# A state space layer's decays: step sizes as logarithms in the exponent, directions merged by a predicated copy out of PSUM

## The chip, the cores and the metric

The kernel runs on one core of a Trainium2 chip. A core has five engines that run their own instruction streams side by side: TensorE (PE, with its weight loads PEld), VectorE (DVE), ScalarE (ACT), GpSimd (POOL) and SyncE (SP, which here issues all DMAs). They wait for each other through semaphores, and each works through its own stream strictly in order. The metric is the time of one execution on the device in microseconds (us).

## The reference

The program is a two-layer encoder over 512 positions of width 1024. Layer 0 mixes tokens by retention and neighbourhood attention, layer 1 by a bidirectional state space (SSD) mixer; a GeGLU block follows each. The change touches only the SSD mixer:

```
dt = softplus(dt_raw + dt_bias)            # per position, direction, head
A = -exp(a_log)
log_a = dt * A
v_f = xh * dt[:, :, 0]                     # forward direction
v_b = xh * dt[:, :, 1]                     # backward direction
y = bidir_scan(qc, kb, v_f, v_b, log_a[:, :, 0], log_a[:, :, 1])
y = y + xh * d_skip
y = y * silu(z)
y = rms_norm per group(y) * norm_g
return y @ w_out

# chunked_scan, one direction, chunks of 128 positions
cs = cumsum(log_a)
decay = exp(where(mask, cs_j - cs_l, -inf))
y_intra = einsum((q k^T) * decay, v)
y_inter = (q . h) * exp(cs)
```

There are 32 heads in 4 groups of 8, head width 64, state width 128. Within a chunk, position j of a head receives from position l the weight (q_j . k_l) exp(cs_j - cs_l) dt_l: from l up to j by the forward direction's cs and dt, from l behind j by the backward direction's. The two halves of this 128x128 matrix never overlap, so one matrix per chunk and head holds both directions.

## The kernel before

The stage of the layer (`mixer1`) works channel-major: weights come in units of 128x1024 by DMA (`wst`), ScalarE casts them to their high part (`whi`, L81), VectorE subtracts it for the low part (`wlo`, L82), and three matmuls (L86 to L88) form one product in near full precision. Projections (`project`) go into the four PSUM buffers of the pool `mm`. A second PSUM pool, `px`, has four buffers as well, and everything else of this layer goes round in them: transposes (`pt`), `pg`, the chunk states (`st`), the part of y from earlier chunks (`pi`), the part from within a chunk (`py`), and the sums of squares (`pss`).

`steps` (L587 to L652) computes dt, the running sums `pf` of the logarithms of the decays and the weights `sw` of the chunk states, with (direction, head) on partitions; it writes `pf` to DRAM (`pd`) and transposes `pf`, `dt` and `sw` into `tok`, positions on partitions. `ddt` is the difference of the two directions' dt.

`head(o, j)` (L730 to L747) builds the matrix of one head, for four chunks at once (128x512). It loads two rows of `pd`, broadcast over the partitions (`pb`, forward and backward). Per chunk, ScalarE forms the forward exponent in `e` (L741), VectorE the backward one and the larger of the two (L742, the right one in each half), and ScalarE the matrix of step sizes `ds` from the triangular mask `um` (L744). Then follow Exp over all four chunks (L745), the product with `gt`, the transposed q k^T of the group (L746), and the product with `ds` (L747). `pair(o, q)` multiplies the matrices of two heads with the tokens (`py`, L782), adds `y` from `inter` (`pi` L762, `ti` L766), multiplies by the silu of `z` (L786), squares (L788), splits the result into `yh` and `yl` (L794, L795) and adds up the squares on POOL (L792). `rms` turns them into `pss` (L802), and `out_tile` projects the group out.

What is written in which order stands in the table `SLOTS`, one row per group: G is the products, s a state, h a head, i `inter`, p a pair, t and n a projection of this or the next group, S and N their silus, o an out projection of the group before, r `rms`. The row of the last group:

```
"t9 G h0 s0 s1 o0 t8 h4 s2 h2 i0 t6 o1 t7 S h1 h3 p0 i1 p1 i2 i3 h5 p2 h6 h7 p3"
```

A scheduler then orders the instructions of each engine by their place in this writing, by the buffers that are free, and by priorities (the splits of weights are moved ahead). The order on each engine is fixed when the kernel is built; on the chip an engine waits where the next instruction's inputs or buffers aren't ready. A tile of a pool waits for the last reader of the tile that had its buffer before.

Of the kernel before, what the change touches and what calls it, by code (L numbers as in the profile page):

```python
# [7 lines left out]
F32 = mybir.dt.float32  # L8
R32 = mybir.dt.float32r
BF16 = mybir.dt.bfloat16  # L10
AF = mybir.ActivationFunctionType
ALU = mybir.AluOpType
PSUM = bass.MemoryType.PSUM
# [2 lines left out]
P = 128  # L16
S = 512
NT = S // P
# [517 lines left out]
SSD_H = NG * HPG  # L536
# [16 lines left out]
def mixer1(E, w_dt, w_fm, cw, dtc, cols, mask, w_out, g_post_row, done):  # L553
# [4 lines left out]
    nc, tc = E.nc, E.tc  # L558
    C = P
    H, H2 = SSD_H, 2 * SSD_H  # L560
    with ExitStack() as ctx:
        pool = lambda name, bufs: ctx.enter_context(tc.tile_pool(name=name, bufs=bufs))
        one, two, four = pool("m1", 1), pool("m1b", 2), pool("m1d", 4)

        few = pool("m1s", 1)
# [4 lines left out]
        um = one.tile([P, P], F32, name="um")  # L570
# [7 lines left out]
            nc.sync.dma_start(xd[t], E.x[:, t, :])  # L578


        tok = one.tile([P, 3, NT, H2], F32, name="tok")
        ddt = one.tile([P, NT, H], F32, name="ddt")
        etot = one.tile([P, H2, NT], F32, name="etot")
        pd = E.dram.tile([H2, S], F32, name="pd")
        yd = E.dram.tile([H2, S], F32, name="yd")
# [1 line left out]
        def steps():  # L587
# [7 lines left out]
            for k in range(KD):  # L595
                c = slice(k * H2, k * H2 + H2)
                E.mm3(ps[:H2], wh[:, c], wl[:, c], E.xh[:, k], E.xl[:, k], k == 0, k == KD - 1)
            bc = few.tile([P, 2], F32, name="bc")
            nc.sync.dma_start(bc, dtc)
            nc.scalar.activation(bc[:, 1:2], bc[:, 1:2], AF.Exp)  # L600
            nc.vector.tensor_scalar(bc[:, 1:2], bc[:, 1:2], -1.0, None, op0=ALU.mult)
# [6 lines left out]
            with tc.tile_pool(name="lp", bufs=1) as lpp:  # L608
                dt = lpp.tile([P, 256], F32, name="dt")
                sw = lpp.tile([P, 256], F32, name="sw")  # L610
                ysc = lpp.tile([P, 256], F32, name="ysc")
                msk = half("msk")
                lp = log1p_exp_neg(E, lambda n: lpp.tile([P, 256], F32, name="lp_" + n), z)
                nc.vector.scalar_tensor_tensor(dt, z, 0.0, lp, op0=ALU.max, op1=ALU.add)
                nc.vector.tensor_scalar(la, dt, bc[:, 1:2], None, op0=ALU.mult)
                nc.vector.memset(msk, 1.0)
                nc.vector.memset(chunks(msk)[:, :, 0:1], 0.0)
                nc.vector.tensor_tensor_scan(pf, msk, la, 0.0, op0=ALU.mult, op1=ALU.add)
                ones = lpp.tile([P, P], F32, name="ones")
                diag = lpp.tile([P, 2, P], F32, name="diag")  # L620
                tot = lpp.tile([P, 2, 1], F32, name="tot")
                nc.vector.tensor_copy(tot, chunks(pf)[:, :, C - 1:C])
                for i in range(2):
                    r = slice(i * H2 + H, i * H2 + H2)
                    nc.vector.tensor_tensor(pf[r], pf[r], la[r], op=ALU.subtract)
                nc.vector.tensor_tensor(chunks(tm), tot.broadcast_to([P, 2, C]), chunks(pf), op=ALU.subtract)
                et = lpp.tile([P, 2], F32, name="et")
                nc.scalar.activation(et, tot.rearrange("p c o -> p (c o)"), AF.Exp)

                nc.vector.memset(ones, 1.0)  # L630
                for c in range(2):
                    nc.vector.tensor_scalar(diag[:, c], E.ident, et[:, c:c + 1], None, op0=ALU.mult)
                pe = E.px.tile([P, 2, P], F32, name="pe", tag="px")
                nc.tensor.matmul(pe.rearrange("p c n -> p (c n)"), ones, diag.rearrange("p c n -> p (c n)"),
                                 start=True, stop=True)
                nc.scalar.copy(etot.rearrange("p h (i c) -> p c i h", i=2), pe.rearrange("p c (i h) -> p c i h", i=2))
                for i in range(2):
                    r = slice(i * H2, i * H2 + H2)
                    nc.sync.dma_start(pd[:, i * 256:i * 256 + 256], pf[r])
                    f, b = slice(i * H2, i * H2 + H), slice(i * H2 + H, i * H2 + H2)  # L640
                    nc.scalar.activation(ysc[f], pf[f], AF.Exp)
                    nc.scalar.activation(ysc[b], tm[b], AF.Exp)
                    nc.scalar.activation(sw[f], tm[f], AF.Exp)
                    nc.scalar.activation(sw[b], pf[b], AF.Exp)
                    nc.sync.dma_start(yd[:, i * 256:i * 256 + 256], ysc[r])
                nc.vector.tensor_tensor(sw, sw, dt, op=ALU.mult)
                for i, s in enumerate((pf, dt, sw)):
                    pt = E.px.tile([P, 2, 2, H2], F32, name="pt", tag="px")
                    for c in range(2):
                        nc.tensor.transpose(pt[:, c].rearrange("p i h -> p (i h)"), s[:, c * C:(c + 1) * C], E.ident)  # L650
                    nc.scalar.copy(tok[:, i].rearrange("p (i c) h -> p c i h", i=2), pt)
            nc.vector.tensor_tensor(ddt, tok[:, 1, :, :H], tok[:, 1, :, H:], op=ALU.subtract)  # L652

        def rows(i, dr, g, c):
            o = dr * H + g * HPG
            return tok[:, i, c, o:o + HPG].rearrange("p (h o) -> p h o", o=1).broadcast_to([P, HPG, 64])
# [55 lines left out]
        def state(o, dr, i):  # L712

            g = o["g"]
            c = i if dr == 0 else NT - 1 - i
            xs = E.tmp.tile([P, 512], F32, name="xs", tag="tmp")
            nc.vector.tensor_tensor(hv(xs), hv(o["x"][:, c]), rows(2, dr, g, c), op=ALU.mult)
            ps = E.px.tile([P, 512], F32, name="st", tag="px")
            nc.tensor.matmul(ps, o["bt"][:, c], xs, start=True, stop=True)  # L719
            ns = one.tile([P, 512], F32, name=f"state{dr}{i}")  # L720
# [9 lines left out]
        def head(o, j):  # L730

            g = o["g"]
            h = g * HPG + j
            pb = [three.tile([P, S], F32, name="pb", bufs=3) for _ in range(2)]
            for dr in range(2):
                nc.sync.dma_start(pb[dr], pd[dr * H + h].partition_broadcast(P))
            e = three.tile([P, NT, C], F32, name="e")
            ds = ys.tile([P, NT, C], F32, name="ds")
            for c in range(NT):
                cc = slice(c * C, (c + 1) * C)  # L740
                nc.scalar.activation(e[:, c], pb[0][:, cc], AF.Identity, scale=-1.0, bias=tok[:, 0, c, h:h + 1])  # L741
                nc.vector.scalar_tensor_tensor(e[:, c], pb[1][:, cc], tok[:, 0, c, H + h:H + h + 1], e[:, c],  # L742
                                               op0=ALU.subtract, op1=ALU.max)
                nc.scalar.activation(ds[:, c], um, AF.Identity, scale=ddt[:, c, h:h + 1], bias=tok[:, 1, c, H + h:H + h + 1])  # L744
            nc.scalar.activation(e, e, AF.Exp, scale=-1.0)  # L745
            nc.vector.tensor_tensor(e, e, o["gt"], op=ALU.mult)  # L746
            o["m"][j] = e, nc.vector.tensor_tensor(e, e, ds, op=ALU.mult)  # L747

        def inter(o, q):

# [228 lines left out]
def _layouts(np, i):  # L979
# [19 lines left out]
    cw = np.concatenate([i["c_conv_w"][0], i["c_conv_b"][0][None]])  # L999
    xw, bw, cw = cw[:, :2048].reshape(6, NG, 4, P), cw[:, 2048:2560].reshape(6, NG, 1, P), cw[:, 2560:].reshape(6, NG, 1, P)  # L1000
    a["c_cw"] = np.concatenate([bw, cw, xw], 2).transpose(3, 1, 2, 0)
    a["c_dtc"] = np.tile(np.stack([i["c_dt_bias"][0].reshape(-1), i["c_a_log"][0].reshape(-1)], 1), (2, 1))
    d = np.repeat(i["c_d_skip"][0].reshape(4 * NG, 2), 64, 1)
    a["c_cols"] = np.stack([d.T, i["c_norm_g"][0].reshape(4 * NG, P).T], 1)
    a["c_mask"] = np.triu(np.ones((P, P), np.float32))
# [37 lines left out]
```

## Time and profile before

| | us |
|---|---|
| time, median of 3 runs | 1435.91 (1434.77 to 1436.99) |
| the profiled execution's own time | 1435.64 |
| its span, first to last instruction | 1433.9 |
| the SSD mixer in it | about 655 to 1065 |

TensorE's mean granted clock is 0.994 of full speed. Over the layer's stretch, 655 to 1066 us, TensorE is busy 396.6 us of 411, VectorE 355.5 and ScalarE 283.7. The page of the profile counts 1486 instructions on VectorE and 1192 on ScalarE in the whole program, 128 of each of the three per-chunk operations of `head` among them. Matmuls of 128x512 are pipelined: one shows 0.39 us, while the next starts 0.23 us after it, so busy times on TensorE are a union of overlapping spans. In rows of the timeline the first number is the start, the second the duration, and the brackets name how long the engine had been idle and what ended that.

### The profile page before, as it was taken

The page shows a single profiled execution, that of the slowest core. Times are in us where ns is not written, and L with a number is a line of the kernel's source. Part 1 is how long each engine was busy: PE and PEld are TensorE (multiplying, and loading weights), DVE is VectorE, ACT ScalarE, POOL GpSimd, SP SyncE. Part 2 cuts the span into 40 slices and gives each one's busy share as a digit, 9 for nine tenths or more (in the row PEclk, how much of TensorE's full clock was granted, in tenths as well). Part 3 has the DMA queues.
Part 4 walks back from the last instruction along what each step waited for, and adds up shares of the span by engine and source line. Part 5 has one row for each costly group of instructions (what it writes and reads, how often), then busy time and mean ns, then how long its engine had stood idle before and what let it go on. Part 6 is the DMA issues. An engine that isn't in the chain of part 4 may idle for free.

```text
span 1433.9 us, 18004 instructions
## 1 busy us (share of the span) xinstructions
PE 1400.5 (98%) x6832; PEld 1144.0 (80%) x6832; DVE 945.2 (66%) x1486; ACT 718.4 (50%) x1192; POOL 61.4 (4%) x67
## 2 busy tenths in 40 slices
PE   7999999999999999999999999999889999999998
PEld 6877777898888888888778787777678888888886
DVE  6478888666566552457789886998986666564232
ACT  4346666444444431334887866676644444443230
POOL 0010110100000000000000000000110000000000
PEclk9999999999999999999999999999999999999999
DMA  7443232232332333423565354354532333323221
GB/s 283 148 132 101 85 96 77 86 105 89 103 93 99 101 93 100 131 84 107 144 190 172 121 172 142 93 153 154 152 114 83 100 101 91 103 90 102 88 103 59
DMA packets 56950, 166.34 MB, mean 116 GB/s; under 512 B 7200, under 2 KB 7968, under 8 KB 56864
## 3 DMA queue, kind: packets, MB, share of 16 engines
q1 hardware_dynamic: 56864, 165.20, 36.4%
q8 instruction: 54, 0.88, 0.2%
q14 instruction: 32, 0.26, 0.1%
HBM read 157.57 MB, written 5.51 MB: 114 GB/s over the span
## 4 chain that ended last, share of the span: by engine, by line
PE 88%; DVE 4%; ACT 3%; DMA 2%; issue 2%; POOL 0%; SPq 0%; DVEq 0%; POOLq 0%; ACTq 0%
PE mm L86 27%; PE mm L87 26%; PE mm L88 26%; PE pi L762 1%; DMA pb<-pd 1%; PE st L719 1%; PE py L782 1%; PE pt L140 1%; PE y L449 1%; PE sc L433 1%; DVE wlo L82 0%; PE pt L663 0%; PE sc L434 0%; DMA x<-in_x 0%; ACT whi L81 0%
## 5 line engine op out<-in xcount | busy, mean ns | idle before, releaser
L88 PE MATMUL mm<-xl,whi 128*128 128x512 f32 (+2 forms) x1216 | 463.4, 381 | 3.0 <-DVE xl L82 3.0
L86 PE MATMUL mm<-xh,whi 128*128 128x512 f32 (+1 forms) x1216 | 464.5, 382 | 1.4 <-ACT bf L692 1.2
L87 PE MATMUL mm<-xh,wlo 128*128 128x512 f32 (+2 forms) x1216 | 462.8, 381 | 0.0
L82 DVE TENSOR_TENSOR wlo<-wst,whi 128x1024 fp32r<-128x1024 f32 (+1 forms) x208 | 256.0, 1231 | 125.2 <-ACT whi L81 120.6
L81 ACT CAST whi<-wst 128x1024 fp32r<-128x1024 f32 (+1 forms) x208 | 216.5, 1042 | 125.9 <-PE mm L87 96.3
L88 PEld LDWEIGHTS mm<-xl,whi 128*128 128x128 f32 (+1 forms) x1216 | 229.0, 188 | 47.2 <-DVE xl L82 3.2
L86 PEld LDWEIGHTS mm<-xh,whi 128*128 128x128 f32 x1216 | 229.2, 188 | 46.2 <-ACT bf L692 1.6
L87 PEld LDWEIGHTS mm<-xh,wlo 128*128 128x128 f32 (+1 forms) x1216 | 229.0, 188 | 42.7 <-issue 0.6
L227 DVE SCALAR_TENSOR_TENSOR cv<-mm,cwt,cv 128x511 f32<-128x511 f32 x88 | 66.0, 750 | 148.9 <-ACT cv L226 148.9
L226 ACT ACTIVATE cv<-mm,cwt 128x512 f32<-128x512 f32 x88 | 68.7, 780 | 128.0 <-PE mm L88 128.0
L86 PE MATMUL mm<-whi,hh 128*128 128x512 f32 x288 | 112.0, 389 | 0.0
L87 PE MATMUL mm<-whi,hl 128*128 128x512 f32 x288 | 112.0, 389 | 0.0
L88 PE MATMUL mm<-wlo,hh 128*128 128x512 f32 x288 | 112.0, 389 | 0.0
L81 ACT CAST hh<-cv 128x512 fp32r<-128x512 f32 x44 | 27.3, 621 | 103.3 <-DVE cv L235 103.3
L228 DVE SCALAR_TENSOR_TENSOR cv<-mm,cwt,cv 128x511 f32<-128x511 f32 x88 | 66.0, 750 | 3.0
L86 PEld LDWEIGHTS mm<-whi,hh 128*128 128x128 f32 x288 | 54.1, 188 | 11.3
L87 PEld LDWEIGHTS mm<-whi,hl 128*128 128x128 f32 x288 | 54.1, 188 | 11.2
L88 PEld LDWEIGHTS mm<-wlo,hh 128*128 128x128 f32 x288 | 54.1, 188 | 11.2
L744 ACT ACTIVATE ds<-um,tok,ddt 128x128 f32<-128x128 f32 x128 | 55.3, 486 | 11.9 <-DVE e L747 11.8
L741 ACT ACTIVATE e<-pb,tok 128x128 f32<-128x128 f32 x128 | 43.1, 392 | 16.6 <-DMA pb<-pd 14.6
L82 DVE TENSOR_TENSOR hl<-cv,hh 128x512 fp32r<-128x512 f32 x44 | 30.5, 693 | 28.9 <-ACT hh L81 28.9
L683 DVE SCALAR_TENSOR_TENSOR xf<-mm,cwt,xf 128x511 f32<-128x511 f32 (+1 forms) x64 | 47.2, 741 | 3.1 <-ACT xf L680 2.9
(236 smaller groups left out, 1932.8 us busy)
## 6 DMA issues: line engine op xcount, KB each, us to landing
wst<-in_f_up SPq DMA_DIRECT2D x88, 512.0 KB
wst<-in_f_down SPq DMA_DIRECT2D x44, 512.0 KB
wst<-in_c_fm SPq DMA_DIRECT2D x40, 512.0 KB
pb<-pd SPq DMA_DIRECT2D x64, 256.0 KB
wst<-in_ab_fm SPq DMA_DIRECT2D x20, 512.0 KB
gain<-yd SPq DMA_DIRECT2D x32, 256.0 KB
wst<-in_c_out SPq DMA_DIRECT2D x16, 512.0 KB
gain<-in_norms SPq DMA_DIRECT2D x8, 512.0 KB
```

What stands on the lines that cost most here:

```text
L81: self.nc.scalar.copy(hi, src)
L82: self.nc.vector.tensor_tensor(lo, src, hi.bitcast(F32), op=ALU.subtract)
L86: mm(out, lh, rh, start=first, stop=False)
L87: mm(out, ll, rh, start=False, stop=False)
L88: mm(out, lh, rl, start=False, stop=last)
L140: nc.tensor.transpose(pt[:, j], xs[:, j * P:(j + 1) * P], self.ident)
L226: nc.scalar.activation(o, ps, AF.Identity, scale=w(1), bias=w(3))
L227: nc.vector.scalar_tensor_tensor(o[:, 1:], ps[:, :S - 1], w(0), o[:, 1:], op0=ALU.mult, op1=ALU.add)
L228: nc.vector.scalar_tensor_tensor(o[:, :S - 1], ps[:, 1:], w(2), o[:, :S - 1], op0=ALU.mult, op1=ALU.add)
L683: nc.vector.scalar_tensor_tensor(r[:, a], ps[:, b], wc(j), r[:, a], op0=ALU.mult, op1=ALU.add)
L741: nc.scalar.activation(e[:, c], pb[0][:, cc], AF.Identity, scale=-1.0, bias=tok[:, 0, c, h:h + 1])
L744: nc.scalar.activation(ds[:, c], um, AF.Identity, scale=ddt[:, c, h:h + 1], bias=tok[:, 1, c, H + h:H + h + 1])
```

## The change

In `steps` the step sizes are floored at 1e-20, their logarithm is taken (a new activation, Ln), and `sign * pf + ln dt` is formed, with the sign -1 for the forward and +1 for the backward direction, which comes as a third column with the biases. This sum and `sw` are the two planes of `tok` that are left; `dt` itself and `ddt` are no longer transposed or formed. In `head` ScalarE now adds the token's column to the broadcast rows, once per direction and chunk: the backward exponent in place in its `pb`, the forward one into a PSUM tile `ea` of the pool `px`. One predicated copy on VectorE overwrites the backward exponent with the forward one where the mask `um`, read as integers, isn't zero. Exp and the product with `gt` follow; the product with `ds` is gone, since dt is in the exponent. `pb` has five buffers for three. Operations per head: ScalarE eight of 128x128 and one Exp, as before; VectorE one copy and one product of 128x512 for four operations of 128x128 and two of 128x512.

```diff
-        tok = one.tile([P, 3, NT, H2], F32, name="tok")
-        ddt = one.tile([P, NT, H], F32, name="ddt")
+
+        tok = one.tile([P, 2, NT, H2], F32, name="tok")
...
-            bc = few.tile([P, 2], F32, name="bc")
+            bc = few.tile([P, 3], F32, name="bc")
...
-                for i, s in enumerate((pf, dt, sw)):
+                ex = lpp.tile([P, 256], F32, name="lp_e")
+                nc.vector.tensor_scalar(ex, dt, 1e-20, None, op0=ALU.max)
+                nc.scalar.activation(ex, ex, AF.Ln)
+                nc.vector.scalar_tensor_tensor(ex, pf, bc[:, 2:3], ex, op0=ALU.mult, op1=ALU.add)
+                for i, s in enumerate((ex, sw)):
...
-            nc.vector.tensor_tensor(ddt, tok[:, 1, :, :H], tok[:, 1, :, H:], op=ALU.subtract)
...
-            nc.vector.tensor_tensor(hv(xs), hv(o["x"][:, c]), rows(2, dr, g, c), op=ALU.mult)
+            nc.vector.tensor_tensor(hv(xs), hv(o["x"][:, c]), rows(1, dr, g, c), op=ALU.mult)
...
-            pb = [three.tile([P, S], F32, name="pb", bufs=3) for _ in range(2)]
+            pb = [three.tile([P, NT, C], F32, name="pb", bufs=5) for _ in range(2)]
             for dr in range(2):
                 nc.sync.dma_start(pb[dr], pd[dr * H + h].partition_broadcast(P))
+
+            first = E.px.tile([P, NT, C], F32, name="ea", tag="px")
+            for dr in (1, 0):
+                for c in range(NT):
+                    nc.scalar.activation((first, pb[1])[dr][:, c], pb[dr][:, c], AF.Identity, scale=1.0 - 2 * dr,
+                                         bias=tok[:, 0, c, dr * H + h:dr * H + h + 1])
+            nc.vector.copy_predicated(pb[1], um.bitcast(U32).rearrange("p (o l) -> p o l", o=1).broadcast_to([P, NT, C]), first)
             e = three.tile([P, NT, C], F32, name="e")
-            ds = ys.tile([P, NT, C], F32, name="ds")
-            for c in range(NT):
-                cc = slice(c * C, (c + 1) * C)
-                nc.scalar.activation(e[:, c], pb[0][:, cc], AF.Identity, scale=-1.0, bias=tok[:, 0, c, h:h + 1])
-                nc.vector.scalar_tensor_tensor(e[:, c], pb[1][:, cc], tok[:, 0, c, H + h:H + h + 1], e[:, c],
-                                               op0=ALU.subtract, op1=ALU.max)
-                nc.scalar.activation(ds[:, c], um, AF.Identity, scale=ddt[:, c, h:h + 1], bias=tok[:, 1, c, H + h:H + h + 1])
-            nc.scalar.activation(e, e, AF.Exp, scale=-1.0)
-            nc.vector.tensor_tensor(e, e, o["gt"], op=ALU.mult)
-            o["m"][j] = e, nc.vector.tensor_tensor(e, e, ds, op=ALU.mult)
+            nc.scalar.activation(e, pb[1], AF.Exp)
+            o["m"][j] = e, nc.vector.tensor_tensor(e, e, o["gt"], op=ALU.mult)
...
-    a["c_dtc"] = np.tile(np.stack([i["c_dt_bias"][0].reshape(-1), i["c_a_log"][0].reshape(-1)], 1), (2, 1))
+    sign = np.repeat(np.array([-1, 1], np.float32), SSD_H)
+    a["c_dtc"] = np.tile(np.stack([i["c_dt_bias"][0].reshape(-1), i["c_a_log"][0].reshape(-1), sign], 1), (2, 1))
```

The lines of the changed kernel stand a few further down (L741 and L744 become L745, L745 becomes L749, L746 becomes L750, the copy is L747, and from there on three are added). What the change moves on the engines is read from the built order at three places.

**ScalarE, first heads of group 0**, ahead of the first `py`. Before: the last operations of the third head, two casts, the table of Exp, three Exps, and the silus of `z`.

```order
L744 ACTIVATE ds<-um,tok,ddt 128x128
L81 CAST whi<-wst 128x1024
L741 ACTIVATE e<-pb,tok 128x128 x4
L81 CAST whi<-wst 128x1024
L745 ACT_TABLE_LOAD
L745 ACTIVATE e<-e 128x512 x3
L689 ACT_TABLE_LOAD
L689 ACTIVATE z<-mm 128x512
```

Now, at the same place:

```order
L745 ACTIVATE pb<-pb,tok 128x128 x3
L745 ACTIVATE ea<-pb,tok 128x128 x8
L82 CAST whi<-wst 128x1024
L749 ACT_TABLE_LOAD
L749 ACTIVATE e<-pb 128x512 x2
L745 ACTIVATE pb<-pb,tok 128x128 x4
L693 ACT_TABLE_LOAD
L693 ACTIVATE z<-mm 128x512
```

The eight writes of `ea` for two heads stand in a block ahead of a cast and of Exp, and the third head's Exp has moved behind the silus.

**ScalarE, end of group 2**, where the last pair's square goes to `pss`. Before, ten operations of two heads stand ahead of the square:

```order
L680 ACTIVATE xf<-mm,cwt 128x512
L81 CAST whi<-wst 128x1024
L744 ACTIVATE ds<-um,tok,ddt 128x128 x8
L741 ACTIVATE e<-pb,tok 128x128 x2
L788 ACTIVATE sq<-y 128x512
L794 ACTIVATE yh<-y,col 128x512
L81 CAST whi<-wst 128x1024
```

Now:

```order
L749 ACTIVATE e<-pb 128x512
L82 CAST whi<-wst 128x1024
L745 ACTIVATE pb<-pb,tok 128x128 x4
L82 CAST whi<-wst 128x1024
L791 ACTIVATE sq<-y 128x512
L797 ACTIVATE yh<-y,col 128x512
L693 ACT_TABLE_LOAD
```

Four operations of one head are left there, ahead of a cast.

**ScalarE, tail of group 3**, from the last silus of `z` on. Before, the last Exp stands ahead of the silus' table, and no head is left behind them:

```order
L745 ACTIVATE e<-e 128x512
L689 ACT_TABLE_LOAD
L689 ACTIVATE z<-mm 128x512
L692 ACTIVATE z<-mm 128x512 x3
L788 ACTIVATE sq<-y 128x512
L81 CAST whi<-wst 128x1024
L788 ACTIVATE sq<-y 128x512
L794 ACTIVATE yh<-y,col 128x512 x2
L788 ACTIVATE sq<-y 128x512
L794 ACTIVATE yh<-y,col 128x512
L788 ACTIVATE sq<-y 128x512
L794 ACTIVATE yh<-y,col 128x512
```

Now, behind the four silus, a square, a cast of `wo`, one `ea`, a square and two `yh`:

```order
L745 ACTIVATE ea<-pb,tok 128x128
L82 CAST whi<-wst 128x1024
L745 ACTIVATE ea<-pb,tok 128x128 x2
L749 ACT_TABLE_LOAD
L749 ACTIVATE e<-pb 128x512
L745 ACTIVATE pb<-pb,tok 128x128 x4
L745 ACTIVATE ea<-pb,tok 128x128 x8
L791 ACTIVATE sq<-y 128x512
L797 ACTIVATE yh<-y,col 128x512
L749 ACTIVATE e<-pb 128x512 x2
L791 ACTIVATE sq<-y 128x512
L797 ACTIVATE yh<-y,col 128x512
```

Most of head 5 and all of heads 6 and 7 now stand behind the silus of `z`, with a table load of Exp of their own. Across the program ScalarE loads a table 38 times, 36 before.

More of the change, by code (lines that the diff above doesn't have):

```diff
@@ L10 @@
 BF16 = mybir.dt.bfloat16
+U32 = mybir.dt.uint32
 AF = mybir.ActivationFunctionType
```

## The prediction

> **What bounds the kernel now.** I read the page's busy shares first, then the table of windows for the state space layer (655 to 1065 us, the only stage that the diff touches), then TensorE's waits in it, then the groups by line, and last the timeline round each wait.
>
> The page's busy shares (share of the span, instructions), and the first line of its chain of waits:
>
> ```profile
> PE 1400.5 (98%) x6832; PEld 1144.0 (80%) x6832; DVE 945.2 (66%) x1486; ACT 718.4 (50%) x1192; POOL 61.4 (4%) x67
> ...
> PE 88%; DVE 4%; ACT 3%; DMA 2%; issue 2%; POOL 0%; SPq 0%; DVEq 0%; POOLq 0%; ACTq 0%
> ```
>
> A row of the table of windows: stretch, its length, busy us of TensorE, its weight loads, VectorE, ScalarE and POOL, granted clock, DMA share and GB/s:
>
> ```profile
> 920.00:940.00 20.00, 20.00 (x112) 16.21 (x108) 19.99 (x31) 14.55 (x27) 1.30 (x1) 1.00 0.75 227
> ```
>
> TensorE's waits in this layer: what it waited for, us in total, times, the longest:
>
> ```profile
> PE py L782 <- DVE e L747: 2.8, 1, 2.8
> PE py L782 <- DVE ti L766: 2.1, 2, 1.8
> ...
> PE pss L802 <- POOL sq L792: 1.4, 1, 1.4
> ...
> PE mm L87 <- DVE yl L795: 1.1, 2, 0.6
> ```
>
> TensorE is the bound: 98% busy, 88% of the chain that ended last. From 920 to 940 VectorE is busy 19.99 us of 20, and TensorE still 20.00. So a microsecond taken off VectorE is worth nothing by itself; what the change can win is TensorE's waits on this layer's decays: 2.8 + 2.1 + 1.4 + 1.1 = 7.4 us, and what the clock adds to them, in windows right behind the waits that end at 722.46, 966.61 and 1025.51:
>
> ```profile
> 723.10:726.40 3.30, 3.30 (x22) 2.97 (x17) 2.51 (x4) 1.99 (x6) 0.00 (x0) 0.50 0.46 145
> 968.90:972.10 3.20, 3.20 (x9) 2.48 (x8) 1.89 (x3) 2.93 (x6) 0.09 (x1) 0.50 0.49 138
> ...
> 1026.90:1030.20 3.30, 3.12 (x18) 2.11 (x18) 3.30 (x4) 1.93 (x4) 2.33 (x1) 0.50 0.62 168
> ```
>
> Behind each of the three longest waits stands a stretch at clock 0.50. Over 3.3 us at half speed at most 1.65 us is lost. The ceiling is thus about 7.4 + 3 x 1.65 = 12 us, under 1% of the span. The Trainium skill, "TensorE: Matmul & The Clock Gate", section "What's actually happening", lets the clock fall to half after an idle window of about 3.4 us; here waits of 1.4 to 2.8 us were enough, so the trace decides. By the page's rule those stretches would be worth nothing to the sum.
>
> **The change, head by head.** 32 heads, by the groups of ScalarE and then VectorE in this layer (count | busy us, mean ns of one | idle before them and its cause):
>
> ```profile
> L81 ACT CAST whi<-wst 128x1024 fp32r<-128x1024 f32 x54 | 56.3, 1044 | 9.4 <-PE mm L88 4.2 <-PE mm L87 3.3 <-issue 1.1
> L744 ACT ACTIVATE ds<-um,tok,ddt 128x128 f32<-128x128 f32 x128 | 55.3, 486 | 11.9 <-DVE e L747 11.8
> L741 ACT ACTIVATE e<-pb,tok 128x128 f32<-128x128 f32 x128 | 43.1, 392 | 16.6 <-DMA pb<-pd 14.6 <-PE py L782 2.0
> ```
>
> ```profile
> L82 DVE TENSOR_TENSOR wlo<-wst,whi 128x1024 fp32r<-128x1024 f32 x53 | 65.6, 1238 | 4.6 <-ACT whi L81 4.5
> ...
> L742 DVE SCALAR_TENSOR_TENSOR e<-pb,tok,e 128x128 f32<-128x128 f32 x128 | 39.1, 353 | 4.8 <-DMA pb<-pd 4.8
> L747 DVE TENSOR_TENSOR e<-e,ds 128x512 f32<-128x512 f32 x32 | 21.6, 681 | 0.1
> L746 DVE TENSOR_TENSOR e<-e,gt 128x512 f32<-128x512 f32 x32 | 21.4, 682 | 4.4 <-ACT e L745 4.4
> L795 DVE SCALAR_TENSOR_TENSOR yl<-y,col,yh 128x512 fp32r<-128x512 f32 x16 | 17.2, 1089 | 0.7 <-ACT yh L794 0.7
> ...
> L785 DVE TENSOR_TENSOR y<-py,y 128x512 f32<-128x512 f32 x16 | 10.8, 683 | 0.8 <-PE py L782 0.8
> ```
>
> VectorE spends (39.1 + 21.6 + 21.4) / 32 = 2.57 us a head now; afterwards one multiply, 0.68, and one predicated copy of 128x512 with its data in PSUM. No row has such a copy. Bounds: 0.35 us (the small row above) and 1.09 us (yl, the dearest row of that size). The nearest row is L785, same size, one operand in PSUM: I take 0.68. So 1.36 us, 1.2 less a head, 39 us in all, nearly all of it under TensorE's cover.
>
> ScalarE swaps four ds of 486 ns for four of the L741 kind at 392 that write PSUM. No row writes PSUM from ScalarE; I take 0.32 (the step of a row of L741 back to back) to 0.42 us each, since each ea waits for the one before it in the same PSUM tile. That is 0 to 0.6 us a head less. The new cost is a place: ea takes one of the four "px" buffers of PSUM, which pi, py, st and pss share, from its first write to the predicated copy. SP gets no new kind of work: with five pb buffers the loads of two heads are issued without a wait, which shortens ScalarE's 14.6 us of waiting for pb; at a DMA share of 0.75 and less there is room for them. ScalarE's wait was hidden, so: 0.
>
> **Steps section.** Two transposes of 0.11 us fewer on TensorE: -0.2. The Ln needs a table load of its own, and Exp another one after it. Both stand on ScalarE where it waited 1.83 us for pf:
>
> ```profile
> 690.58 0.42 ACT L641 ACTIVATE ysc<-pf 32x256 f32<-32x256 f32 x1 [1.83 <-DVE pf L618]
> ```
>
> The second load (1.28) and the Ln (about 0.42 as this row) fit into 1.83: 0; if they don't, what is late is a cast of whi, +1 at most.
>
> **First heads of group 0.** The timeline there (start, us, engine, line, operation; in brackets the idle time before it and what ended it):
>
> ```profile
> 710.80 0.68 DVE L727 TENSOR_TENSOR state<-st,state 128x512 f32<-128x512 f32 x1
> ...
> 715.29 1.28 ACT L745 ACT_TABLE_LOAD   x1
> ...
> 716.59 1.15 ACT L745 ACTIVATE e<-e 128x512 f32<-128x512 f32 x2
> ...
> 719.03 0.39 PE L87 MATMUL mm<-xh,wlo 128*128 128x512 f32 x1
> 719.26 0.39 PE L88 MATMUL mm<-xl,whi 128*128 128x512 f32 x1
> ...
> 722.46 1.45 PE L782 MATMUL py<-e,xt 128*64 128x128 f32 x16 [2.81 <-DVE e L747]
> ...
> 723.84 2.84 PE L762 MATMUL pi<-cf,state 128*128 128x128 f32 x12
> ```
>
> After the change the first ea must wait for a px buffer that a state addition frees, about 711.5 (710.80 + 0.68). Then 8 x 0.42, a cast of 1.04 and the table load of 1.28: the two Exps run 717.2 to 718.4, and the second multiply ends at 719.1. TensorE arrives at 719.6 (722.46 - 2.81). The wait goes, and with it up to 1.4 us of half clock (twelve pi take 2.84 us at clock 0.50, so half of it at full speed): -2 to -4, taken -3.
>
> **Ends of groups 1 and 2.** The timeline at the end of group 2, ahead of its pss:
>
> ```profile
> 960.70 3.19 ACT L744 ACTIVATE ds<-um,tok,ddt 128x128 f32<-128x128 f32 x8
> ...
> 962.96 0.68 DVE L786 TENSOR_TENSOR y<-y,z 128x512 f32<-128x512 f32 x1
> ...
> 963.80 0.69 ACT L741 ACTIVATE e<-pb,tok 128x128 f32<-128x128 f32 x2
> 964.39 0.62 ACT L788 ACTIVATE sq<-y 128x512 f32<-128x512 f32 x1
> ...
> 965.15 1.41 POOL L792 TENSOR_TENSOR sq<-sq 128x512 f32<-128x512 f32 x1 [19.45 <-ACT sq L788]
> 966.61 1.05 PE L802 MATMUL pss<-mean,sq 128*128 128x1 f32 x8 [1.40 <-POOL sq L792]
> ```
>
> Here y stood ready at 963.64 (962.96 + 0.68), but eight ds and two e were queued ahead of its square: 0.75 us. After the change four pb and a cast are left ahead of it (the second place of the order), which need not wait for y; and 20 matmuls instead of 17 lie between py and pss, 0.23 us each (the two matmuls above). Group 1 goes the other way, 15 matmuls instead of 24. Together I take -1.5 (0 to -3).
>
> **New waits for px.** In groups 1 and 2 the pi of a pair now take buffers that an ea gives back. A pi that is late by one predicated copy costs 0.3 to 0.7 us; behind it on TensorE stand the projections' matmuls, so it is paid in full. Two or three such: +1 (0.5 to 2).
>
> **Tail of group 3.** This decides the sign. The timeline from the last silus of z to pss:
>
> ```profile
> 1021.30 1.28 ACT L689 ACT_TABLE_LOAD   x1
> ...
> 1024.06 1.57 ACT L692 ACTIVATE z<-mm 128x512 f32<-128x512 f32 x3
> ...
> 1025.50 0.65 ACT L788 ACTIVATE sq<-y 128x512 f32<-128x512 f32 x1
> 1025.51 1.09 PE L782 MATMUL py<-e,xt 128*64 128x128 f32 x16 [1.75 <-DVE ti L766]
> ...
> 1026.97 1.98 PE L782 MATMUL py<-e,xt 128*64 128x128 f32 x16 [0.37 <-DVE ti L766]
> 1027.48 1.34 ACT L794 ACTIVATE yh<-y,col 128x512 fp32r<-128x512 f32 x2
> ...
> 1040.63 0.95 PE L802 MATMUL pss<-mean,sq 128*128 128x1 f32 x8
> ```
>
> Before, no Exp stands behind the silu's table load at 1021.30, and both py wait only for a px buffer, which ti frees behind the silu of z. Now the ea of heads 5 to 7 need such buffers too, so they stand behind that silu on ScalarE, and Exp must be loaded once more. Added up from 1025.50: sq 0.5, wo 0.5, ea 0.4, sq 0.5, two yh 1.3, ea 0.4, whi 1.05, two ea 0.8, table load 1.28, Exp 0.6: 1032.8. VectorE has y 0.55, wo 0.68 and wlo 1.22 between the copy (behind the last ea, done 1031.6) and the multiply, which ends at 1034.8: py of pair 2 is 9.3 us late. ScalarE's four pb (1.3) and eight ea (3.3) end at 1037.4. The square waits for py 1.7, y + py 0.68 and y times z 0.68, to 1037.9; with yh it is 1039.1, after two Exps 1040.3, after the multiply 1041.0. Then py 1.7, y + py 0.68, y times z 0.68, sq 0.6 and POOL's sum 1.4: pss at 1046.1 against 1040.63, +5.5. The out matmuls (38 before pss then, 36 now) fill TensorE's wait and are no gain. Bounds: +3.5 (ea at 0.32, the wlo late) to +7.5 (copies at 1.09, a pi more in the way). If the first ea got their buffers before the silu, it would be 0.
>
> The Trainium skill, "ScalarE: Activation LUTs", section "What ACT_TABLE_LOAD costs", speaks against this change: a switch of tables costs 1283 ns and a drain of about 1380 more. The trace has the 1283 ns, and no drain: 715.29 + 1.28 is 716.57, and the Exp starts at 716.59. With the page's drain the sum would be an estimated 1.4 us higher.
>
> **Sum**, against the profiled execution's 1435.64: -0.2 - 3 - 1.5 + 1 + 5.5 = +1.8. The median of the runs is 0.27 above that execution, so I forecast 1435.91 + 1.8 = **1437.7 us**.
>
> **Rivals.** (1) Faster: the tail doesn't stretch. VectorE is 1.2 us a head quicker, so px buffers come free sooner and the last ea get theirs before the silu; ScalarE's order is fixed, which speaks against it. 1437.7 - 5.5 = 1432.2, and 1430 with the ends at their best. (2) Slower: ScalarE's queue stops at an ea that has no buffer, with casts of whi behind it. It decides as soon as a stop outlasts the matmuls whose weights are split already, a unit of 12 at 0.23 us being 2.8 us. A stop of twice that, 5.6, costs 2.8 us; one in each of groups 1 and 2: 1437.7 + 5.6 = 1443.3. For it: there are four px buffers, and two can be held by ea. Against it: casts of whi wait for TensorE to give back buffers (9.4 us idle, 7.5 of it put down to matmuls), so they run ahead now. (3) It does nothing: the new waits eat what the first heads give, the tail pays half: 1435 to 1437.
>
> **Chances.** Forecast 0.45 (its own range 1434.5 to 1441), rival 1 0.25, rival 2 0.2, rival 3 0.1. Range 1430 to 1445. A measurement of this kernel tells about 0.2% from no change, 2.9 us: faster is under 1433.0, slower over 1438.8. Faster 0.25 (rival 1 mostly); same 0.37 (0.24 of the forecast, rival 3, and the rest of rival 1); slower 0.38 (0.18 of the forecast, rival 2).
>
> **What will show it.** The wait of py at 722 gone, its twelve pi in about 1.4 us; the predicated copy at 0.68 us in its group; one more Exp table load behind the last silu of z, py of pair 3 some 14 us later, and pss about 5.5 us later after the end of the last z projection. Wrong, if ea in group 3 run ahead of the silu, if the copy costs over 1.1 us, or if casts of whi gain idle time put down to VectorE.

## The result, and the profile after

The changed kernel takes 1445.69 us, the median of 5 runs (1442.88 to 1448.37), against 1435.91 (1434.36 to 1437.08) of the kernel before: a ratio of 1.0072, 95% interval 1.0058 to 1.0086. It is slower by about 10 us, above the range of the forecast.

The profiled execution took 1446.27 us, its span is 1444.5 (before 1433.9), 10.6 us more. TensorE's timeline shows where they arose, at places that both kernels have:

| first matmul of | before | after | difference | gained since the place above |
|---|---|---|---|---|
| pss, group 0 | 787.84 | 785.40 | -2.44 | -2.44 |
| pg, group 2 | 896.58 | 897.68 | +1.10 | +3.54 |
| pi behind the last z projection | 1023.37 | 1025.01 | +1.64 | +0.54 |
| pss, group 3 | 1040.63 | 1049.85 | +9.22 | +7.58 |
| end of the span | 1433.9 | 1444.5 | +10.6 | +1.38 |

The page's busy shares of the kernel after: TensorE does the same work, VectorE 31.8 us less (945.2 before), ScalarE 7.4 less.

```profile
PE 1403.4 (97%) x6830; PEld 1143.9 (79%) x6830; DVE 913.4 (63%) x1359; ACT 711.0 (49%) x1194; POOL 60.7 (4%) x67
```

The groups of the new operations, in the layer (count | busy us, mean ns | idle before them and its cause), ScalarE and then VectorE:

```profile
L745 ACT ACTIVATE ea<-pb,tok 128x128 f32<-128x128 f32 x128 | 43.9, 361 | 4.5 <-DVE state L731 1.9 <-issue 1.7
L745 ACT ACTIVATE pb<-pb,tok 128x128 f32<-128x128 f32 x128 | 43.5, 391 | 25.1 <-DMA pb<-pd 25.1
```

```profile
L747 DVE COPY_PREDICATED pb<-um,ea 128x512 f32<-128x512 uint32 x32 | 23.2, 739 | 3.8 <-ACT ea L745 3.8
```

The prices were about as taken: 739 ns for the predicated copy (taken 0.68 us), 361 for an ea (taken 0.32 to 0.42). What had not been taken is in the second row: ScalarE now waits 25.1 us for loads of pb, 14.6 before. TensorE's waits in the layer after (total us, times, longest):

```profile
PE mm L87 <- ACT yh L797: 6.1, 2, 3.7
PE pss L805 <- POOL sq L795: 6.0, 3, 2.7
...
PE py L785 <- DVE e L750: 1.9, 3, 0.8
PE st L723 <- ACT state L726: 1.6, 1, 1.6
```

The waits for the decays of the first heads (2.8) and for ti (2.1) are gone. The four rows shown come to 15.6 us in their place, for yh, for sums of squares (pss waited 1.4 before), for products of VectorE and for a state copy of ScalarE. Behind five of the waits the clock halves, for three in the rows of the prediction (the stretch, its length, busy us, granted clock, DMA share, GB/s):

```profile
884.20:887.50 3.30, 3.30 (x10) 2.55 (x9) 0.76 (x2) 0.00 (x0) 0.98 (x1) 0.50 0.08 31
973.00:976.20 3.20, 3.20 (x9) 2.52 (x8) 1.34 (x2) 1.38 (x3) 1.47 (x1) 0.50 0.43 157
1031.00:1034.20 3.20, 3.13 (x7) 2.48 (x8) 3.20 (x9) 2.48 (x4) 0.00 (x0) 0.50 0.71 239
1041.20:1044.50 3.30, 3.02 (x7) 2.46 (x8) 2.75 (x4) 1.27 (x3) 1.04 (x1) 0.50 0.00 0
1051.50:1054.70 3.20, 3.20 (x9) 2.45 (x9) 1.40 (x2) 0.65 (x2) 0.70 (x1) 0.50 0.00 0
```

The timeline of the tail, after:

```profile
1025.70 1.57 ACT L696 ACTIVATE z<-mm 128x512 f32<-128x512 f32 x3
...
1028.16 0.40 ACT L745 ACTIVATE ea<-pb,tok 128x128 f32<-128x128 f32 x1
...
1032.25 1.28 ACT L749 ACT_TABLE_LOAD   x1
1034.28 0.63 ACT L749 ACTIVATE e<-pb 128x512 f32<-128x512 f32 x1 [0.75 <-DVE pb L747]
1036.50 1.28 ACT L745 ACTIVATE pb<-pb,tok 128x128 f32<-128x128 f32 x4 [1.58 <-DMA pb<-pd]
1037.69 2.39 ACT L745 ACTIVATE ea<-pb,tok 128x128 f32<-128x128 f32 x8
```

And TensorE there:

```profile
1029.77 0.50 PE L87 MATMUL mm<-whi,yh 128*128 128x512 f32 x1 [3.71 <-ACT yh L797]
...
1037.60 1.09 PE L785 MATMUL py<-e,xt 128*64 128x128 f32 x16
...
1041.48 0.80 PE L87 MATMUL mm<-whi,yh 128*128 128x512 f32 x1 [2.36 <-ACT yh L797]
...
1045.17 1.09 PE L785 MATMUL py<-e,xt 128*64 128x128 f32 x16
...
1049.85 1.05 PE L805 MATMUL pss<-mean,sq 128*128 128x1 f32 x8 [2.68 <-POOL sq L795]
```

It is the chain of the forecast, head 5 and then heads 6 and 7 behind the silus of z, with three waits of TensorE.

### The profile page after: what moved, and what is told of

It is laid out like the page before. It is cut to its first block, busy times and chain, and to the rows that moved or that the text cites. A ratio compares the mean times of both kernels' runs of the same rounds, so it can differ in the third digit from the quotient of the medians.

```text
span 1444.5 us, 17883 instructions
## 1 busy us (share of the span) xinstructions
PE 1403.4 (97%) x6830; PEld 1143.9 (79%) x6830; DVE 913.4 (63%) x1359; ACT 711.0 (49%) x1194; POOL 60.7 (4%) x67
## 4 chain that ended last, share of the span: by engine, by line
PE 42%; DMA 2%; DVE 2%; ACT 2%; issue 1%; POOL 1%; DVEq 0%; SPq 0%; POOLq 0%; ACTq 0%
PE mm L87 13%; PE mm L88 13%; PE mm L89 13%; DMA pb<-pd 2%; PE pi L765 1%; PE st L723 1%; PE py L785 1%; DMA wst<-in_c_fm 1%; PE pt L667 0%; ACT ea L745 0%; ACT pb L745 0%; ACT whi L82 0%; DVE x L176 0%; POOL sq L795 0%; DVE xs L132 0%
## 5 line engine op out<-in xcount | busy, mean ns | idle before, releaser
L745 ACT ACTIVATE pb<-pb,tok 128x128 f32<-128x128 f32 x128 | 43.5, 391 | 25.1 <-DMA pb<-pd 25.1
L687 DVE SCALAR_TENSOR_TENSOR xf<-mm,cwt,xf 128x510 f32<-128x510 f32 (+1 forms) x64 | 47.3, 743 | 13.0 <-ACT xf L684 12.7
L87 PE MATMUL mm<-whi,yh 128*128 128x512 f32 x112 | 46.2, 412 | 6.1 <-ACT yh L797 6.1
```

What stands on the lines that cost most here:

```text
L87: mm(out, lh, rh, start=first, stop=False)
L687: nc.vector.scalar_tensor_tensor(r[:, a], ps[:, b], wc(j), r[:, a], op0=ALU.mult, op1=ALU.add)
L745: nc.scalar.activation((first, pb[1])[dr][:, c], pb[dr][:, c], AF.Identity, scale=1.0 - 2 * dr, bias=tok[:, 0, c, dr * H + h:dr * H + h + 1])
```

## The experiments

Ratios are to the kernel before, run on the same chip in the same session, with their 95% intervals. "Tail" is the time from the start of the last z projection's last matmul to the last group's pss: 17.5 us before, 25.1 after. Two theories of the loss were open. The first: ea takes a place in PSUM that pi, py and pss need, and the order that follows puts heads behind the silus. The second: the backward exponent is written back into its pb, which is held until Exp has read it, so the next heads' loads come late, and ScalarE waits for them in its one queue with other work behind.

**ea in SBUF.**

```diff
-            first = E.px.tile([P, NT, C], F32, name="ea", tag="px")
+            first = ys.tile([P, NT, C], F32, name="ea")
```

> The tile ea moves from the PSUM pool px into SBUF (the two buffers that ds had left); nothing else is edited. Theory (ea competes with pi, py and pss for the four px buffers, and that puts the last heads behind the silus of z): the tail's 7.6 us and the half-clock stretch behind it (1.4) go, and the order at the end of group 1 is as before, so 3 more: 1433 to 1437 us. Rival (the last heads are late because their pb loads are late, whatever ea lies in): the time stays at 1443 to 1446.

Measured: 1439.48 us, ratio 1.0034 (1.0021 to 1.0048); tail 17.3. So the place in PSUM makes the tail, and moving it takes back about half of the loss. At the end of group 1, 24 matmuls stand between py and pss again, as before the change, the square starts 0.03 us after its y, and TensorE doesn't wait. The time was outside both expectations. The timeline of this run ahead of group 2's pss shows what is left:

```profile
958.34 0.99 ACT L745 ACTIVATE ea<-pb,tok 128x128 f32<-128x128 f32 x3 [1.94 <-DMA pb<-pd]
959.04 0.68 DVE L789 TENSOR_TENSOR y<-y,z 128x512 f32<-128x512 f32 x1
959.48 1.28 ACT L745 ACTIVATE pb<-pb,tok 128x128 f32<-128x128 f32 x4 [0.15 <-DMA pb<-pd]
...
962.56 0.63 ACT L791 ACTIVATE sq<-y 128x512 f32<-128x512 f32 x1
...
965.09 1.28 PE L805 MATMUL pss<-mean,sq 128*128 128x1 f32 x8 [3.32 <-POOL sq L795]
```

y is ready at 959.72, and its square starts at 962.56, behind two heads' exponents that had waited for loads. TensorE pays 3.3 us, for 1.4 in the kernel before.

**Heads 5 to 7 written ahead of i2 and i3** in the last group, ea still in PSUM.

```diff
-    "t9 G h0 s0 s1 o0 t8 h4 s2 h2 i0 t6 o1 t7 S h1 h3 p0 i1 p1 i2 i3 h5 p2 h6 h7 p3",
+    "t9 G h0 s0 s1 o0 t8 h4 s2 h2 i0 t6 o1 t7 S h1 h3 p0 i1 p1 h5 h6 h7 i2 i3 p2 p3",
```

> Only the last group's row of the table of slots: h5 h6 h7 are written ahead of i2 and i3; ea stays in PSUM. Theory (the tail is a matter of order alone): pss of the last group comes some 17 us after its last z projection as before, not 24.8, and the time falls by 7.5 to 9 us to 1436.7 to 1438.2; what is left over the kernel before, 1 to 2 us, is the end of group 1. Rival (PSUM is short by one buffer in any order): pi and py now wait in turn, and the time is 1441 or more.

Measured: 1443.9, ratio 1.0060 (1.0041 to 1.0080); tail 17.5. The tail is repaired as expected, and the time hardly falls: the last matmul of the z projections starts at 1033.74 instead of 1024.78, and 3.2 us of these 9.0 had arisen by group 2's pss. Behind that, the largest single wait of TensorE is 2.05 us at 1012.99, with a window of half clock behind it. Its chain begins with ScalarE's wait for a load and runs over a cast and a split of weights to x, the sum that the out projection adds to (L828):

```profile
1008.28 0.99 ACT L745 ACTIVATE pb<-pb,tok 128x128 f32<-128x128 f32 x3 [1.77 <-DMA pb<-pd]
...
1009.98 1.03 ACT L82 CAST whi<-wst 128x1024 fp32r<-128x1024 f32 x1
1011.05 1.23 DVE L83 TENSOR_TENSOR wlo<-wst,whi 128x1024 fp32r<-128x1024 f32 x1 [0.54 <-ACT whi L82]
1012.19 0.75 DVE L828 SCALAR_TENSOR_TENSOR x<-mm,rg,x 128x512 f32<-128x512 f32 x1
1012.99 0.50 PE L87 MATMUL mm<-whi,yh 128*128 128x512 f32 x1 [2.05 <-DVE x L828]
```

The tail's waits have been exchanged for earlier ones. The time is in the rival's range, but the trace puts this longest wait down to a load, not to a place in PSUM: neither theory alone covers it.

**The sums of squares of group 1 later**, so that 25 matmuls stand between py and pss, for 15.

```diff
-n9 N i3 n8 h7 p3 n4 r n5 N",
+n9 N i3 n8 h7 p3 n4 n5 r N",
```

> Only group 1's row of the table of slots: the sums of squares (r) are written behind n5, which puts 25 matmuls between the last py and pss for 15. Theory (15 matmuls, 3.4 us, don't cover the chain from py to the sums on POOL): the wait of 2.0 us and the half-clock stretch behind it (1.5) go: 1442.0 to 1442.7 us. Rival (the wait returns at the next operation that needs the same result): within 1 us of 1445.7.

Measured: 1444.19, ratio 1.0057 (1.0036 to 1.0078). In the trace the wait ahead of group 1's pss (1.82 us) and the half clock at 884 are gone, as expected, though the square is still 1.7 us late. The time lies between the two expectations, and its interval overlaps that of the changed kernel: a saving of 3 us is consistent, and not shown by the times.

**Seven pb buffers.**

```diff
-            pb = [three.tile([P, NT, C], F32, name="pb", bufs=5) for _ in range(2)]
+            pb = [three.tile([P, NT, C], F32, name="pb", bufs=7) for _ in range(2)]
```

> Only the buffers of pb: seven for five. Theory (ScalarE's queue stands 25 us for loads of pb, and what stands behind them there, state copies, Exps and squares, makes TensorE wait at 710.6, 963.8 and 971.2): those three waits of 1.7, 0.8 and 1.7 us shrink, 1441 to 1444 us. Rival (more buffers only let loads of pb go ahead of the weights in SP's order): the waits move to casts of whi and the time stays or grows, 1445 to 1449.

Measured: 1447.12, ratio 1.0083 (1.0062 to 1.0104), and ScalarE waits 28.6 us for pb. The three waits are 1.4, 0.4 and 1.3 us, hardly shorter. The time is in the rival's range, but ScalarE stands idle ahead of the casts of whi no longer than in the changed kernel (18.4 us for 20.3), so the rival's mechanism isn't shown either. More buffers alone don't help.

**The backward exponent into e**, three pb buffers, ea in PSUM.

```diff
-            pb = [three.tile([P, NT, C], F32, name="pb", bufs=5) for _ in range(2)]
+            pb = [three.tile([P, NT, C], F32, name="pb", bufs=3) for _ in range(2)]
...
+            e = three.tile([P, NT, C], F32, name="e")
...
-                    nc.scalar.activation((first, pb[1])[dr][:, c], pb[dr][:, c], AF.Identity, scale=1.0 - 2 * dr,
+                    nc.scalar.activation((first, e)[dr][:, c], pb[dr][:, c], AF.Identity, scale=1.0 - 2 * dr,
...
-            nc.vector.copy_predicated(pb[1], um.bitcast(U32).rearrange("p (o l) -> p o l", o=1).broadcast_to([P, NT, C]), first)
-            e = three.tile([P, NT, C], F32, name="e")
-            nc.scalar.activation(e, pb[1], AF.Exp)
+            nc.vector.copy_predicated(e, um.bitcast(U32).rearrange("p (o l) -> p o l", o=1).broadcast_to([P, NT, C]), first)
+            nc.scalar.activation(e, e, AF.Exp)
```

> The backward exponent is written into e, not back into its pb, so that both pb are free as soon as ScalarE has read them, and three pb buffers do; ea stays in PSUM. Theory A (a pb that is held until Exp makes the next loads late, a cost of its own): ScalarE's 25 us of waiting for pb fall towards the 15 of before, the waits at 710, 964 and 971 us shrink, and the time is 1441 to 1444; the tail stays at 24 to 25 us from the last z projection to pss. Theory B (only the place in PSUM costs): 1445 to 1447.

Measured: 1453.32, ratio 1.0135 (1.0114 to 1.0156): a miss of both. The group of e on ScalarE in this run:

```profile
L746 ACT ACTIVATE e<-pb,tok 128x128 f32<-128x128 f32 x128 | 42.7, 391 | 41.7 <-DMA pb<-pd 41.7
```

The waiting for loads grew to 41.7 us. A pb is held not only by a backward exponent in it; the forward pb is held as long as its ea has no place in PSUM. (With the same three buffers and ea in SBUF, further down, it is 8.7.) So the same places were tried with `bufs=5` left as it was:

> The backward exponent in e, ea in PSUM, and five pb buffers as in the changed kernel. Theory (with three buffers it was the forward pb, held until ea has a place in PSUM, that made loads late: 41.7 us of ScalarE's waiting; five make up for it, and only the place in PSUM is left): ScalarE waits 15 to 25 us for pb, the tail stays, 1442 to 1446. Rival (e itself, taken from its five buffers earlier, is what cost 9 us): 1449 to 1453.

Measured: 1446.11, ratio 1.0081 (1.0067 to 1.0096); 19.0 us of waiting for pb, tail 25.9. With ea in PSUM the backward exponent's place makes no difference that the intervals show, and three buffers are too few.

**Both places changed**: ea in SBUF, the backward exponent in e, four pb buffers. The edit is that of the run just above (the backward exponent in e), and besides

```diff
-            pb = [three.tile([P, NT, C], F32, name="pb", bufs=5) for _ in range(2)]
+            pb = [three.tile([P, NT, C], F32, name="pb", bufs=4) for _ in range(2)]
-            first = E.px.tile([P, NT, C], F32, name="ea", tag="px")
+            first = ys.tile([P, NT, C], F32, name="ea")
```

> Both edits: ea in SBUF and the backward exponent in e, four pb buffers. If late loads are what the kernel with ea in SBUF (1439.5) still loses, the square ahead of group 2's pss isn't held up any more, and the time is 1434 to 1437. If it loses elsewhere, 1438.5 to 1440.5 as with ea in SBUF alone.

Measured: 1431.66, ratio 0.9976 (0.9965 to 0.9987): faster than the kernel before, and than either expectation. ScalarE waits 6.4 us for pb. The square ahead of group 2's pss is 1.1 us late, for 2.8 with ea in SBUF alone, and TensorE waits 1.2 there. The same with `bufs=3`, and with `bufs=5`:

> ea in SBUF, the backward exponent in e, and only three pb buffers. Theory (pb are short only where a place in PSUM or the way back into pb holds them): within 2 us of the same with four, 1430 to 1434. Rival (the number of pb buffers counts by itself): 1436 or more.

> ea in SBUF, the backward exponent in e, five pb buffers as in the changed kernel, so that only the two places differ from it. Theory (loads aren't late any more, so a fifth buffer brings nothing): 1430 to 1433.5. Rival (each buffer lets loads go ahead and is worth some): 1428 to 1430.

Measured: 1428.88, ratio 0.9964 (0.9952 to 0.9977), and 1430.28, ratio 0.9965 (0.9954 to 0.9976). The number of buffers no longer makes a difference that the intervals show. The groups of the run with five:

```profile
L746 ACT ACTIVATE ea<-pb,tok 128x128 f32<-128x128 f32 x128 | 41.6, 393 | 0.1
L746 ACT ACTIVATE e<-pb,tok 128x128 f32<-128x128 f32 x128 | 40.8, 391 | 10.5 <-PE py L785 8.1 <-DMA pb<-pd 2.4
```

**ea in SBUF, the backward exponent in pb, three buffers**, to part the exponent's place from everything else.

```diff
-            pb = [three.tile([P, NT, C], F32, name="pb", bufs=5) for _ in range(2)]
+            pb = [three.tile([P, NT, C], F32, name="pb", bufs=3) for _ in range(2)]
-            first = E.px.tile([P, NT, C], F32, name="ea", tag="px")
+            first = ys.tile([P, NT, C], F32, name="ea")
```

> ea in SBUF, the backward exponent back into its pb, three pb buffers: beside the kernel with the same three buffers and the exponent in e (1428.9), only the place of the backward exponent differs. Theory (a pb held until Exp makes loads late, and the fewer the buffers the more): ScalarE waits 25 us or more for pb, and the time is 1441 to 1450. Rival (the place of the exponent only changes the order, not the loads): near 1439.5 as with five, 1437 to 1440.

Measured: 1444.62, ratio 1.0060 (1.0046 to 1.0073), ScalarE waits 41.0 us for pb. Beside the 0.9964 of the kernel that differs only in the exponent's place, that is the second theory's effect with ea in SBUF: about 14 us with three buffers, about 10 with five (1.0034 against 0.9965).

**The kernel before with three px buffers.**

```diff
-        self.px = pool("px", 4, space=PSUM)
+        self.px = pool("px", 3, space=PSUM)
```

> The kernel before, with three px buffers for four, nothing else. Theory (the layer has no px buffer to spare): 1439 to 1446, with new waits of TensorE for st, pi and py. Rival (three do as well, and only the order that ea brings is at fault): 1435 to 1437.

Measured: 1437.97, ratio 1.0024 (1.0013 to 1.0035). One px buffer less costs about 3.4 us, between both expectations. Where they arise the trace doesn't tell: its execution was the fastest of the run (1434.86), and pi's wait of 2.0 us for ti in the last group only replaces py's of 2.1. The place of ea in the round costs the layer about 5.5 us with the backward exponent in pb (1.0072 against 1.0034), and about 17 with it in e and five buffers (1.0081 against 0.9965), far more than a buffer taken out altogether.

**The logarithm alone**: no ds and no second product, but the directions merged as before by the larger of the negated exponents, which picks the wrong one near the diagonal where the two step sizes differ much. The signs in `steps` are turned round for it, and `pb` has three buffers. In `head`:

```diff
...
+            for c in range(NT):
+                nc.scalar.activation(e[:, c], pb[0][:, c], AF.Identity, scale=-1.0, bias=tok[:, 0, c, h:h + 1])
+                nc.vector.scalar_tensor_tensor(e[:, c], pb[1][:, c], tok[:, 0, c, H + h:H + h + 1], e[:, c],
+                                               op0=ALU.add, op1=ALU.max)
+            nc.scalar.activation(e, e, AF.Exp, scale=-1.0)
```

> The logarithm of the step sizes without the predicated copy: the two directions are merged as before, by the larger of the two negated exponents, so the wrong direction wins near the diagonal where the step sizes differ much, and the result is only near the reference. No ds, one product less on VectorE, no ea. Theory (the exponents are no loss, all of it comes with the copy out of PSUM): 1431 to 1435. Rival (the order that follows from fewer operations is what loses): 1438 or more.

Measured: 1432.58, ratio 0.9982 (0.9971 to 0.9993). This version gains 1 to 4 us, also because ScalarE has four operations a head less; so the logarithm isn't what loses. Nor is it the predicated copy itself, since its versions with both places changed gain as much: the loss comes with the places of its data.

The predicated copy's versions side by side, with ScalarE's waits for pb in each trace:

| ea | backward exponent | pb buffers | ratio (95%) | waits for pb, us | tail, us |
|---|---|---|---|---|---|
| PSUM | pb | 5 (the change) | 1.0072 (1.0058 to 1.0086) | 25.1 | 25.1 |
| PSUM | pb | 7 | 1.0083 (1.0062 to 1.0104) | 28.6 | 27.1 |
| PSUM | e | 3 | 1.0135 (1.0114 to 1.0156) | 41.7 | 25.6 |
| PSUM | e | 5 | 1.0081 (1.0067 to 1.0096) | 19.0 | 25.9 |
| SBUF | pb | 3 | 1.0060 (1.0046 to 1.0073) | 41.0 | 17.3 |
| SBUF | pb | 5 | 1.0034 (1.0021 to 1.0048) | 20.8 | 17.3 |
| SBUF | e | 3 | 0.9964 (0.9952 to 0.9977) | 8.7 | 18.1 |
| SBUF | e | 4 | 0.9976 (0.9965 to 0.9987) | 6.4 | 17.3 |
| SBUF | e | 5 | 0.9965 (0.9954 to 0.9976) | 2.4 | 17.3 |

The two faults don't add up. With ea in PSUM, the backward exponent's place makes no difference with five buffers: the tail stays at 25 to 26 us, and ScalarE waits 19 us for loads also with the exponent in e. Only with both places changed do the loads come in time.

## Why the prediction was wrong

It forecast 1437.7, no change that can be measured, with a range up to 1445; 1445.7 came. In the two traces the forecast +1.8 stands against +10.6. Of the 8.8 us between them, 4.6 lie at the ends of groups 1 and 2 (forecast there -1.5 and +1), 2.1 in the tail, 1.4 behind it and 0.8 in the first heads. Term by term, with the table of places:

- **First heads and steps section**, taken -3.2: measured -2.44 up to group 0's pss. The wait at 722 is gone, and pi no longer runs at half clock there. A new one of 1.57 us stands at 710.6, for a state copy behind ScalarE's wait of 3.16 us for a load of pb. The size was about right, in part by luck: the second multiply ended at 720.57, 1.5 us later than forecast, and py doesn't wait for it only because TensorE comes later too (721.59, taken 719.6).
- **Ends of groups 1 and 2**, taken -1.5: this step failed. From group 0's pss to the last z projection the kernel lost 4.1 us, 3.5 of them up to the end of group 1. The forecast saw that 15 matmuls stand between py and pss in group 1, for 24, and set them against 20 for 17 in group 2, without pricing the chain that they have to cover: y, square, sum on POOL. Its assumption that the four pb left ahead of a square "need not wait for y" was right and beside the point, since they wait for their loads. The timeline of group 1's end, after:

```profile
873.81 0.63 ACT L749 ACTIVATE e<-pb 128x512 f32<-128x512 f32 x1
...
874.47 0.33 SPq L740 DMA_DIRECT2D pb<-pd  x1
...
876.29 1.09 PE L785 MATMUL py<-e,xt 128*64 128x128 f32 x16
...
877.80 0.99 ACT L745 ACTIVATE pb<-pb,tok 128x128 f32<-128x128 f32 x3 [3.36 <-DMA pb<-pd]
...
878.16 0.69 DVE L789 TENSOR_TENSOR y<-y,z 128x512 f32<-128x512 f32 x1
...
880.29 0.63 ACT L791 ACTIVATE sq<-y 128x512 f32<-128x512 f32 x1
...
882.83 1.05 PE L805 MATMUL pss<-mean,sq 128*128 128x1 f32 x8 [1.82 <-POOL sq L795]
```

  From py to pss 6.5 us pass, and 15 matmuls cover 3.4. The square starts 1.4 us after y is ready at 878.85, because three pb, an xf and a cast stand ahead of it behind a load. TensorE waits 1.8 us and then runs 3.3 us at half clock, at most 1.65 lost, which together make the 3.5. Both parts are needed for so long a wait, and the order comes with ea's place. With ea in SBUF, 24 matmuls stand there and TensorE doesn't wait, though the backward exponent is in pb; with ea in PSUM and the exponent in e, 14 matmuls stand there and it waits 1.2, with the square 0.6 late; and with 25 matmuls it doesn't wait, with the square 1.7 late. In group 2 the square is 1.8 us late, behind a wait of 1.7 us for a load of weights, and TensorE waits 1.5 there, about as long as before; 0.8 more come from a py that waits for its e at 963.82.
- **Loads of pb**, taken 0: its reasons didn't hold. The forecast said that five buffers would shorten ScalarE's waiting, and that there was room on the DMA. The waiting rose from 14.6 to 25.1 us, and two things show. Buffers are held longer, a backward pb through the copy and Exp, a forward one until ea has its place. In the timeline just shown, the load that ScalarE waits 3.36 us for is issued at 874.47, right behind the Exp that read the buffer (873.81 + 0.63). And SP's issue of pb loads waited 90.6 us in all for ea, 50.3 with ea in SBUF. In the first heads loads crowd each other: five pb and four gain loads are issued from 697.6 to 705.5, where the kernel before had sent three of each by 701.5 and the next pb at 706.0. From 700 to 710 the DMA share is 1.01, for 0.74 before, and ScalarE waits 3.16 us for one of them. The holding is shown by runs (20.8 us of waiting against 2.4 where only the backward exponent's place differs); what the crowding adds to the 25.1 no run shows by itself. This unasked question, how long each buffer is held and what its loads meet, lengthens the step above; the runs with both places changed wait 2.4 to 8.7 us.
- **New waits of pi for px**, taken +1: no wait of pi for a predicated copy of any length shows in the trace.
- **Tail**, taken +5.5 (bounds 3.5 to 7.5): the mechanism was right, and the size 7.6. The term was mis-sized by what the chain meets on its way: Exp of head 5 waits 0.75 us for its copy, the first py starts 0.6 us and the last 1.2 us after its product is done, behind out matmuls, of which seven ahead of the last py ran at half clock. The wait of 1.58 us for a load of pb costs nothing here: the eight ea behind it end at 1040.08, and the y that the next square needs is ready at 1040.15. Another 1.4 us came behind pss, where a window of half clock that the sum didn't have slows the out projection.

Rival 2 (1443.3) came nearest in time, yet by another mechanism: ScalarE's queue was stopped mostly by loads (25.1 us) and little by ea without a buffer (4.5 us idle before ea in all), and what stood behind were squares, a state copy and Exps rather than casts. Of the forecast's three signs of being wrong none appeared: the ea of group 3 didn't run ahead of the silu, the copy took 0.74 us, and the casts of whi did gain idle time (20.3 us for 9.4), but put down to matmuls (17.2) and loads. No sign watched the loads of pb.

The Trainium skill, "ScalarE: Activation LUTs", section "Step-by-step: what each stage is for", says that ScalarE writes to PSUM faster than to SBUF, with the caveat that it is of use only if TensorE doesn't need most of PSUM. A single ea agrees, 361 ns in PSUM against 391 in SBUF. But in a row the next one starts after 0.3 us at either place, and the 128 of them keep ScalarE busy 43.9 us in PSUM and 42.3 in SBUF, so no time of ScalarE is saved. The caveat shows: the place costs the layer 5 us and more (1.0072 against 1.0034).

## What to carry to other kernels

Ask of each edit not only how long its operations take but how long they hold each buffer, and what fills that buffer next; writing a result back into a tile that a DMA had filled ties the next load to the end of the chain. A tile that joins a full round of PSUM buffers must find its place among all that use the round, and the orders that follow on an engine with one queue can cost more than the tile's own time. More buffers also mean more loads at once. Where an engine has slack in busy time, a gain is still lost if what TensorE waits for stands behind another wait in that engine's queue: price the chain from the wait's release to TensorE against the matmuls that cover it, for each place by itself.

## What the runs showed of the hardware

- The predicated copy of 128x512 takes 739 ns with its data in PSUM and 750 with it in SBUF: where the data lie makes next to no difference, and it is dearer than a plain operation of that size (682 ns, the product of e and gt) by 8 to 10%. The group with its data in SBUF, with five buffers and both places changed:

```profile
L748 DVE COPY_PREDICATED e<-um,ea 128x512 f32<-128x512 uint32 x32 | 23.7, 750 | 1.9 <-ACT e L746 1.6 <-ACT ea L746 0.2
```

- A switch of ScalarE's table shows 1283 ns and no drain behind it in the trace after either: 717.32 + 1.28 is 718.60, and Exp starts at 718.61.

```profile
717.32 1.28 ACT L749 ACT_TABLE_LOAD   x1
718.61 1.16 ACT L749 ACTIVATE e<-pb 128x512 f32<-128x512 f32 x2
```

- Eight ea in a row take 2.39 us in the tail, a step of 0.3, less than the 0.36 that one takes: they overlap, though all write one PSUM tile. The forecast let each wait for the one before it, and its 0.42 was too much. In the first heads the eight took 2.94; in SBUF they take 2.44.

- The length of a wait alone doesn't tell whether TensorE's clock falls behind it. A wait of 3.02 us for the same operation of VectorE (xl) stands behind the layer in both traces: before, half clock follows from 1064.3 to 1067.6 (granted clock 0.51); after, the clock is 1.00 from 1074.0 to 1077.3. In the trace after, half clock follows a wait of 1.53 us (971.21) and not one of 1.57 (710.57). So the up to 1.65 us that each such stretch costs can't be forecast from the wait, and these are single executions.
